# Score products of full array height: the keys' lo parts stacked twice, and smaller raw weight and temporary buffers

## The chip, the cores and the metric

The kernel runs on one core of a Trainium2 chip. The metric is the device time of one execution in microseconds (us), median of several runs. Engine names are those of the profile: PE (TensorE, its weight loads shown apart as PEld), DVE (VectorE), ACT (ScalarE), POOL (GpSimd) and SP (SyncE, which here only issues DMAs).

## The reference: what is computed

A two-layer backbone over 512 latent tokens and 256 context tokens of 1024 features. Each layer is a half SwiGLU step, an attention mixer with 16 heads of 64 features, and a second half SwiGLU step. Mixer 0 is a neighbourhood attention, mixer 1 a windowed attention with 4 key heads; both also look at all context keys. Everything is float32.

```python
def ffn_sublayer(h, shift, scale, gate, w_in, w_out, g, b):
    y = swiglu(modulate(h, shift, scale), w_in, w_out)
    return layer_norm(ALPHA * h + FFN_RES * gate * y, g, b)
...
        s_win = jnp.einsum('bcqhd,bicjhd->bhcqij', q_r, k_r).astype(jnp.float32) + bias
        s_ctx = jnp.einsum('bcqhd,bkhd->bhcqk', q_r, kc).astype(jnp.float32)
        p = jax.nn.softmax(jnp.concatenate([s_win, s_ctx], axis=-1), axis=-1).astype(v.dtype)
```

## The kernel before

Features lie on the 128 partitions, tokens along the free axis. To keep float32 accuracy with the fast float32r matmul, every large operand x is split in two float32r parts, hi (x rounded) and lo (x minus hi), and a product is a sum of three: hi·hi, hi·lo, lo·hi (`mm3`, lines 115 to 117).

**Weights** come as units of 1 MB (`wunit`). A unit arrives in two halves of 128x1024 in raw tiles `wr` (tag "wr", two of them); from each half two quarters of 128x512 are made: ACT copies the hi part `wh` (line 100), POOL subtracts to get the lo part `wl` (line 101). There are nine `wh` and nine `wl` tiles. All loads stand in one queue, SP's, in program order, and a load waits there until its buffer is free.

**A head has 64 features**, half of the array's 128 rows. The queries of a head are stacked to full height by `stack_q`: hi above lo for the even head of a pair, lo above hi for the odd one. `stack_k` makes, for each head, a tile `nk` (in mixer 1 `wk`) with the hi part of the keys in both halves, and one tile `nkl` (`wkl`) for both heads with their lo parts, each in its own half. A score product is then two matmuls (`scores`, lines 526 and 527; in mixer 1's window 816 and 817): the full-height one, (q_hi + q_lo)·k_hi, and one of half height, 64 rows, q_hi·k_lo:

```python
nc.tensor.matmul(ps, q[:, qc], k[:, kc], start=True, stop=False)
nc.tensor.matmul(ps, q[own, qc], kl[own, kc], start=False, stop=True)
```

Here `own` is the half in which the head's hi part lies. Of such pairs mixer 0 has 160 (`lat`, 128, and `cself`, 32) and mixer 1 has 128, all with 128 query columns as weights and 256 moving key columns, but for 32 of mixer 1 that have 384.

**After the scores** of a head, DVE takes the row minimum (the scores are negated), ACT the exponential, POOL scales (line 565), PE transposes (line 549), ACT or DVE copies out of PSUM, and PE multiplies with the values (line 558). Score banks have the PSUM tag "s", two of them.

**Buffers in SBUF.** Stacked queries and keys, pieces of modulation weights (`wt`, read by DVE's products on line 173) and some temporaries share the tag "slab" with 10 tiles; a quad of mixer 0's heads takes 2 x 5 of them. Temporaries have the tags "t2" (7 tiles) and "ln" (3). In `layer_norm` the squares of the centred tiles go to "ln" tiles, and POOL and DVE add them; the last outputs `ot` use "ln" for feature tiles 0 to 2 and "t2" for the others.

**Order.** The program is written once; a list scheduler with its own model of the engines then orders the instructions on each engine's queue. Each engine runs its queue in order. `bias_tables` puts 8 DMAs `xd` and 16 DMAs `yd` of 252 KB into SP's queue in the second chunk of the first SwiGLU step.

Of the kernel before, what the change touches and what calls it, by code (L numbers as in the profile page):

```python
# [8 lines left out]
F32 = mybir.dt.float32  # L9
# [9 lines left out]
P = 128  # L19
D = 1024  # L20
DT = D // P
NL = 512
# [8 lines left out]
NH = 16  # L31
RW = 63
# [3 lines left out]
def hybrid_kernel(ctx: ExitStack, tc: tile.TileContext, h0, cc, crow, wmod, wmodt, bmod, lnp, wst,  # L36
# [46 lines left out]
    wpos, loaded = [0], [None]  # L83

    def wunit(slabs=False, again=None):
        i = wpos[0] if again is None else again
        if again is None:
            wpos[0] += 1
        hs, ls = [], []
        for s in range(2):  # L90
            raw = wp.tile([P, 1024], F32, tag="wr", name=f"wr{i}_{s}" + ("" if again is None else "b"), bufs=2)
            loaded[0] = nc.sync.dma_start(raw[:], wst[i, :, s * 1024:(s + 1) * 1024])
            for q in range(2):
                nm = f"{i}_{2 * s + q}" + ("" if again is None else "b")
                if slabs:
                    hi, lo = [sp.tile([P, 512], F32R, tag="slab", name=f"w{x}{nm}", bufs=10) for x in "hl"]
                else:
                    hi, lo = [wp.tile([P, 512], F32R, tag=f"w{x}", name=f"w{x}{nm}", bufs=9) for x in "hl"]
                src = raw[:, q * 512:(q + 1) * 512]
                nc.scalar.copy(hi[:], src)  # L100
                nc.gpsimd.tensor_tensor(out=lo[:], in0=src, in1=hi[:].bitcast(F32), op=ALU.subtract)  # L101
                hs.append(hi)
                ls.append(lo)
# [21 lines left out]
    def gemv(layer, ch, pieces, tag):  # L125
        """silu(c) @ w_mod + b_mod for 512 columns (chunk ch of the host's layout), both streams, features on partitions."""
        nm = f"{layer}_{ch}"
        ps = bank(tag, f"gm{nm}")
        kt = 0
        for t in pieces:  # L130
            for j in range(t.shape[1]):
                q = kt % 4
                nc.tensor.matmul(ps[32 * q:32 * q + 32, :], c_sb[:, kt, :], t[:, j, :], start=kt < 4, stop=kt >= 4,
                                 tile_position=(0, 32 * q))
                kt += 1
        ev = t2(f"gev{nm}")
        nc.scalar.copy(ev[:], ps[:])
        pt = bank(tag, f"gt{nm}")
        for j in range(4):
            nc.tensor.matmul(pt[:, 2 * j:2 * j + 2], ev[:, j * P:(j + 1) * P], sel[:], start=True, stop=True)  # L140
        for a in range(2):
            t = ch * 2 + 8 * a if ch < 4 else ch * 4 + 2 * a
            nc.vector.tensor_tensor(out=mod[layer][:, t:t + 2, :], in0=pt[:, 4 * a:4 * a + 4].rearrange("p (t s) -> p t s", s=2),
                                    in1=bmod_sb[:, layer, t:t + 2, None].broadcast_to([P, 2, 2]), op=ALU.add)

    def gemv_bg(layer, ch):
        pieces = []
        for q in range(8):
            t = sp.tile([P, 1, 512], F32, tag="slab", name=f"wm{layer}_{ch}_{q}", bufs=10)
# [6 lines left out]
    def gemv_dve(layer, t0, t1):  # L156
        """the same for feature tiles t0:t1 as rows of products that VectorE sums, in steps that tick() issues"""
        cb = []

        def start():  # L160
            for i in range(4):
                t = sp.tile([P, 512], F32, tag="slab", name=f"cb{layer}_{t0}_{i}", bufs=10)
# [4 lines left out]
        def products(acc, t, half):  # L167
            w = sp.tile([P, 512], F32, tag="slab", name=f"wt{layer}_{t}_{half}", bufs=10)
# [34 lines left out]
    def derive(layer, ln, mlayer, m, q=None):  # L203
        """Scales and biases of the modulated LN output: u = zn*sc + bi, alpha*h = zn*ag + ab."""
# [25 lines left out]
    def rows(t):  # L230
        """512 grid tokens in column-major order, seen in row-major order"""
        return t.rearrange("p (c r) -> p r c", r=8)

    def rowm(t):
        """512 grid tokens in row-major order, as rows and columns"""
        return t.rearrange("p (r c) -> p r c", c=64)

    def mod_out(nm, d, c0, c1, st, prm, rm=False, dd=None):
        """zn (in z) -> u hi/lo (row-major if rm) and alpha*h (in z)"""
# [11 lines left out]
        else:  # L251
            uf = sp.tile([P, 512], F32, tag="slab", name=f"uf{nm}_{d}", bufs=10)
# [10 lines left out]
    def keep(d, c0, c1, prm, rm=False):  # L263
        """z = alpha*h; with rm in row-major order from then on, in the room of the tile before"""
# [12 lines left out]
    def behind(x, y):  # L277
        """issue x after y if they run on the same engine"""
# [7 lines left out]
    def rstd(nm, ve, n):  # L286
        """1/sqrt(ve) by Newton's iteration from a guess on the bits"""
# [14 lines left out]
    def total(nm, n, src, split):  # L302
        """sum of the eight tiles that src(d) gives: the first on Pool, the others on DVE"""
# [16 lines left out]
    def spread(nm, y, n, tag):  # L320
        """[P, n] tile pr with pr[:, j*128 + t] = y[t, j]"""
# [5 lines left out]
    def layer_norm_pe(nm, c0, c1, tags):  # L327
        """layer_norm with TensorE's sums, for when it has nothing else to do"""
# [24 lines left out]
    def layer_norm(nm, c0, c1, tag):  # L353
        """z -> z - mean in place for columns c0:c1; returns a function that multiplies tile d by rstd."""
# [35 lines left out]
    def flush():  # L390
        """the deferred alpha*h"""
# [8 lines left out]
    def ffn(nm, groups, gt, mid, post, units=(), opened={}, head=None, apart=None):  # L400
        """z += gt * swiglu(u); mid() runs first, post(gi) after a group is complete. The first products may be there."""
# [85 lines left out]
    def wo_pairs(nm, w, os, groups, gt, tags, base=0):  # L487
        """z += gt * (o of two pairs of heads, in tiles that begin with column base) @ w_o rows"""
# [16 lines left out]
    def slab(nm):  # L505
        return sp.tile([P, NT], F32R, tag="slab", name=nm, bufs=10)
# [3 lines left out]
    def stack_q(q0, q1, c0, c1, src, scale):  # L510
        """two heads' scaled queries: [hi; lo] for head 0, [lo; hi] for head 1"""
# [5 lines left out]
    def stack_k(k0, k1, kl, c0, c1, src):  # L517
        """two heads' keys: [hi; hi] each, and the lo parts of both"""
        for k, own, other in ((k0, LOW, HIGH), (k1, HIGH, LOW)):
            nc.scalar.copy(k[own, c0:c1], src[own, :])  # L520
# [3 lines left out]
    def scores(h, ps, q, k, kl, qc, kc):  # L524
        own = (LOW, HIGH)[h]
        nc.tensor.matmul(ps, q[:, qc], k[:, kc], start=True, stop=False)
        nc.tensor.matmul(ps, q[own, qc], kl[own, kc], start=False, stop=True)

    def v_tiles(nm, w, js=range(NT // P), tags=("mm",)):
        """value tiles [128 tokens, 256]"""  # L530
# [13 lines left out]
    def transpose(nm, p, order, tags):  # L544
        """tile p = the transposes of its 128-column pieces, in that order"""
# [8 lines left out]
    def pv_mm(po, terms):  # L554
        """po[64h:64h+64] = sum of v^T p^T over key tiles, the two heads side by side; terms[i][h] = (v, p^T)"""
# [32 lines left out]
    def na_mixer(gt, ctx_ln, post):  # L588
        def proj(qd):
            i0 = wpos[0]  # L590
            ws = [None, None]
            qk = [[slab(f"n{x}{qd}_{pr}") for x in ("q0", "q1", "k0", "k1", "kl")] for pr in range(2)]

            def half(pr, c0, c1, again=None):
# [9 lines left out]
                stack_k(*sl[2:5], c0, c1, ps)  # L604
# [26 lines left out]
        def lat(qd, pr, st, oh, ol, cbs=range(4)):  # L631
# [15 lines left out]
            for cb in cbs:  # L647
                pts = []
                qc = slice(cb * P, (cb + 1) * P)
                for h in range(2):  # L650
                    nm = f"{qd}_{pr}_{cb}_{h}"
                    ps = bank("s", f"s{nm}")
                    scores(h, ps[:, 256:512], sl[h], sl[2 + h], sl[4], qc, slice(NL, NT))
                    scores(h, ps[:, 0:256], sl[h], sl[2 + h], sl[4], qc, slice(KS[cb], KS[cb] + 256))
# [17 lines left out]
        def cself(qd, pr, st, oh, ol):  # L672
# [3 lines left out]
            for h in range(2):  # L676
                nm = f"{qd}_{pr}_c_{h}"
                ps = bank("s", f"s{nm}")
                for b in range(2):
                    scores(h, ps[:, b * 256:(b + 1) * 256], sl[h], sl[2 + h], sl[4], slice(NL + b * P, NL + (b + 1) * P),  # L680
# [64 lines left out]
    def wa_mixer(gt, ctx_ln, post):  # L745
# [9 lines left out]
        def rope(nm, ps, scale):  # L755
            """rotary of scale * ps, as a float32 tile"""
# [14 lines left out]
        ks = [[slab(f"wk{x}_{i}") for x in ("0", "1", "l")] for i in range(2)]  # L771
# [23 lines left out]
        def attn(s, q, oh, ol, bs=range(4)):  # L795
# [8 lines left out]
            for b in bs:  # L804
# [8 lines left out]
                for h in range(2):  # L813
                    own = (LOW, HIGH)[h]
                    pb = bank("s", f"sw{nm}_{h}")
                    nc.tensor.matmul(pb[:, 0:nw], q[h][:, qc], k[h][:, k0:k1], start=True, stop=False)
                    nc.tensor.matmul(pb[:, 0:nw], q[h][own, qc], k[2][own, k0:k1], start=False, stop=False)
# [5 lines left out]
                    scores(h, pb2, q[h], k[h], k[2], qc, slice(NL, NT))  # L823
# [73 lines left out]
    def open_av():  # L897
        """banks for the products of chunk 0 that start before all of u is there: [half][group] = (a, v)"""
# [89 lines left out]
def _tokens(a):  # L988
    """(tokens, 1024) -> (128, 8, tokens): features on partitions"""
# [3 lines left out]
def _k_unit(w):  # L993
    """(1024, 256) -> (128, 8*256)"""
# [3 lines left out]
def _r_unit(w):  # L998
    """(256, 1024) -> (128, 4 column quarters, 2 row tiles, 256)"""
# [110 lines left out]
```

## Time and profile before

| what | value |
|---|---|
| median of 3 runs | 2991.55 us (2989.05 to 2994.65) |
| profiled execution: span from first to last instruction | 2994.0 us; no other time of it is listed |
| busy share: PE, PEld, DVE, ACT, POOL | 97%, 84%, 62%, 34%, 42% |
| mean granted TensorE clock | 0.980 |
| first SwiGLU step with the start | 0 to about 620 us |
| mixer 0 | about 620 to 1080 us |
| SwiGLU, SwiGLU | about 1080 to 2230 us |
| mixer 1 | about 2230 to 2567 us |
| last SwiGLU step | about 2567 to 2994 us |

In the timeline a row has the start in us, the duration in us, the engine, the line, the operation, what it writes and reads, and its shape (rows*columns of the array, then partitions x elements of the operand that streams). A duration of a matmul includes its way through the array, so matmuls overlap in the record; what one costs in a full stream is the distance from its start to the start of the next.

### The profile page before, as it was taken

The numbers are of one execution on the slowest core, as the hardware profiler recorded it, in microseconds if no ns is written. First come the engines' busy times: TensorE is split into PE (matmuls) and PEld (weight loads), VectorE is DVE, ScalarE is ACT, GpSimd is POOL, SyncE is SP. The second block draws the span as 40 slices with busy tenths as digits, with TensorE's granted clock in tenths as the row PEclk, the third lists the DMA queues.
The fourth block names the chain that finished last, engine by engine and source line by source line (L and its number), as shares of the span: only waits on it lengthen the run. The fifth ranks groups of instructions, "written<-read, shape, count | busy, mean of one in ns | idle before, by whom it ended". The sixth has DMA issues, their size and how long they took to land. (4 is left out here: it accounts for less than half of the span.)

```text
span 2994.0 us, 48485 instructions
## 1 busy us (share of the span) xinstructions
PE 2900.1 (97%) x18106; PEld 2502.0 (84%) x18106; DVE 1843.8 (62%) x5023; ACT 1009.5 (34%) x2082; POOL 1248.1 (42%) x1102
## 2 busy tenths in 40 slices
PE   8899999999999979999999999999999999899998
PEld 5788888887887869888888888888887677799997
DVE  3498983475444585777775767776267566733335
ACT  4122222364343453121213522222245444533333
POOL 4233333573333454232335633332466343644453
PEclk9999999999999989999999999999998899899998
DMA  7545442221111222343332323332231000233332
GB/s 287 155 137 152 134 131 70 86 96 50 54 54 46 80 74 67 109 124 107 126 106 90 107 89 120 113 120 74 82 97 57 29 29 29 64 92 93 99 106 85
DMA packets 114860, 285.98 MB, mean 96 GB/s; under 512 B 20288, under 2 KB 32704, under 8 KB 113600
## 3 DMA queue, kind: packets, MB, share of 16 engines
q1 hardware_dynamic: 114336, 282.74, 30.1%
q8 instruction: 142, 2.33, 0.3%
q14 instruction: 94, 0.77, 0.1%
q10 hardware_dynamic: 288, 0.14, 0.0%
HBM read 280.74 MB, written 6.48 MB: 96 GB/s over the span
## 5 line engine op out<-in xcount | busy, mean ns | idle before, releaser
L101 POOL TENSOR_TENSOR wl<-wr,wh 128x512 fp32r<-128x512 f32 x632 | 836.4, 1339 | 1245.8 <-ACT wh L100 967.7
L100 ACT CAST wh<-wr 128x512 fp32r<-128x512 f32 x632 | 383.0, 620 | 694.9 <-DMA wr<-in_wst_dram 307.9
L173 DVE CUSTOM_DVE_ANT_0 jk<-wt,cb 128x256 f32<-128x256 f32 x960 | 507.0, 567 | 0.0
L396 DVE SCALAR_TENSOR_TENSOR z<-pd1a,gt,z 128x512 f32<-128x512 f32 (+1 forms) x168 | 103.2, 619 | 83.7 <-PE pd1a L117 83.4
L396 DVE SCALAR_TENSOR_TENSOR z<-pd0a,gt,z 128x512 f32<-128x512 f32 (+1 forms) x168 | 102.9, 619 | 83.6 <-PE pd0a L117 83.0
L396 DVE SCALAR_TENSOR_TENSOR z<-pd0b,gt,z 128x256 f32<-128x256 f32 (+1 forms) x176 | 104.7, 600 | 66.4 <-PE pd0b L117 64.9
L115 PE MATMUL pa0a<-uh,wh 128*128 128x512 f32 (+1 forms) x328 | 113.3, 345 | 11.7 <-ACT wh L100 8.2
L115 PE MATMUL pd0a<-gh0a,wh 128*128 128x512 f32 (+1 forms) x336 | 114.6, 344 | 2.5 <-DVE z L396 2.5
L116 PE MATMUL pd0b<-gl0b,wh 128*128 128x256 f32 (+1 forms) x352 | 116.7, 332 | 0.0
L115 PE MATMUL pd0b<-gh0b,wh 128*128 128x256 f32 (+1 forms) x352 | 116.6, 334 | 0.0
L117 PE MATMUL pd0b<-gh0b,wl 128*128 128x256 f32 (+1 forms) x352 | 116.4, 332 | 0.0
L115 PE MATMUL pa1a<-uh,wh 128*128 128x512 f32 (+1 forms) x336 | 114.5, 341 | 1.3 <-DVE uh L260 1.2
L116 PE MATMUL pv1a<-ul,wh 128*128 128x512 f32 (+1 forms) x336 | 114.3, 340 | 0.0
L115 PE MATMUL pv1a<-uh,wh 128*128 128x512 f32 (+1 forms) x336 | 114.3, 340 | 0.0
L116 PE MATMUL pd0a<-gl0a,wh 128*128 128x512 f32 (+1 forms) x336 | 114.3, 340 | 0.0
L116 PE MATMUL pd1a<-gl1a,wh 128*128 128x512 f32 (+1 forms) x336 | 114.2, 340 | 0.0
L117 PE MATMUL pd0a<-gh0a,wl 128*128 128x512 f32 (+1 forms) x336 | 114.2, 340 | 0.0
L116 PE MATMUL pa1a<-ul,wh 128*128 128x512 f32 (+1 forms) x336 | 114.2, 340 | 0.0
L117 PE MATMUL pa1a<-uh,wl 128*128 128x512 f32 (+1 forms) x336 | 114.1, 340 | 0.0
L117 PE MATMUL pd1a<-gh1a,wl 128*128 128x512 f32 (+1 forms) x336 | 114.0, 340 | 0.0
L117 PE MATMUL pv1a<-uh,wl 128*128 128x512 f32 (+1 forms) x336 | 114.0, 339 | 0.0
L115 PE MATMUL pd1a<-gh1a,wh 128*128 128x512 f32 (+1 forms) x336 | 113.6, 342 | 0.0
(880 smaller groups left out, 9246.3 us busy)
## 6 DMA issues: line engine op xcount, KB each, us to landing
wr<-in_wst_dram SPq DMA_DIRECT2D x316, 512.0 KB
wt<-in_wmodt_dram SPq DMA_DIRECT2D x240, 256.0 KB
wr_0b<-in_wst_dram SPq DMA_DIRECT2D x19, 512.0 KB
wr_1b<-in_wst_dram SPq DMA_DIRECT2D x19, 512.0 KB
wm<-in_wmod_dram SPq DMA_DIRECT2D x8, 1024.0 KB
nb<-yd SPq DMA_DIRECT2D x60, 128.0 KB
wm<-in_wmod_dram SPq DMA_DIRECT2D x16, 256.0 KB
yd<-xd SPq DMA_DIRECT2D x16, 252.0 KB
```

The lines of the kernel that those rows point to most:

```text
L100: nc.scalar.copy(hi[:], src)
L101: nc.gpsimd.tensor_tensor(out=lo[:], in0=src, in1=hi[:].bitcast(F32), op=ALU.subtract)
L115: nc.tensor.matmul(ps, a[0], b[0], start=first, stop=False)
L116: nc.tensor.matmul(ps, a[0], b[1], start=False, stop=False)
L117: nc.tensor.matmul(ps, a[1], b[0], start=False, stop=last)
L173: x = nc.vector.tensor_tensor_reduce(out=junk[:, 0:256], in0=w[:, q * 256:q * 256 + 256], in1=cb[2 * st + half][:, q * 256:q * 256 + 256], ...
L396: last[0] = nc.vector.scalar_tensor_tensor(out=zt(d, c0, c1), in0=pd, scalar=gt[:, d, st:st + 1], in1=zt(d, c0, c1), op0=ALU.mult, op1=ALU ...
```

## The change

It does five things.

1. `stack_k` makes a lo tile for each head (`nl`, in mixer 1 `wkl0`, `wkl1`), and a new ACT copy puts the lo part into the other half as well, so that the lo keys stand there twice. The second matmul of a score product takes all 128 rows: (q_hi + q_lo)·k_lo. The product lo·lo, left out before, is thereby added.
2. A quad of mixer 0 takes 2 x 6 slabs and mixer 1's keys 2 x 4; the tag "slab" has 12 tiles (`SLABS`).
3. A weight unit arrives in four quarters of 128x512, each in a raw tile of its own, three raw tiles in all: 3 x 512 elements a partition instead of 2 x 1024.
4. "t2" has 6 tiles and "ln" has 2.
5. Comments are gone, so some line numbers move: the load of `wr` from 92 to 94, the split from 100 and 101 to 99 and 100, the three products of `mm3` from 115, 116, 117 to 114, 115, 116; the score products stay on 526 and 527.

```diff
-        return tp.tile([P, 512], F32, tag=tag, name=nm, bufs={"t2": 7, "ln": 3, "sl": 2}[tag])
+        return tp.tile([P, 512], F32, tag=tag, name=nm, bufs={"t2": 6, "ln": 2, "sl": 2}[tag])
...
-        for s in range(2):
-            raw = wp.tile([P, 1024], F32, tag="wr", name=f"wr{i}_{s}" + ("" if again is None else "b"), bufs=2)
-            loaded[0] = nc.sync.dma_start(raw[:], wst[i, :, s * 1024:(s + 1) * 1024])
-            for q in range(2):
+        for q in range(4):
+            nm = f"{i}_{q}" + ("" if again is None else "b")
+            raw = wp.tile([P, 512], F32, tag="wr", name=f"wr{nm}", bufs=3)
+            loaded[0] = nc.sync.dma_start(raw[:], wst[i, :, q * 512:(q + 1) * 512])
...
-    def stack_k(k0, k1, kl, c0, c1, src):
-        for k, own, other in ((k0, LOW, HIGH), (k1, HIGH, LOW)):
+    def stack_k(k0, k1, kl0, kl1, c0, c1, src):
+        for k, kl, own, other in ((k0, kl0, LOW, HIGH), (k1, kl1, HIGH, LOW)):
             nc.scalar.copy(k[own, c0:c1], src[own, :])
             nc.scalar.copy(k[other, c0:c1], src[own, :])
             nc.vector.tensor_tensor(out=kl[own, c0:c1], in0=src[own, :], in1=k[own, c0:c1].bitcast(F32), op=ALU.subtract)
+            nc.scalar.copy(kl[other, c0:c1], kl[own, c0:c1].bitcast(F32))
...
-        nc.tensor.matmul(ps, q[own, qc], kl[own, kc], start=False, stop=True)
+        nc.tensor.matmul(ps, q[:, qc], kl[:, kc], start=False, stop=True)
...
-                    nc.tensor.matmul(pb[:, 0:nw], q[h][own, qc], k[2][own, k0:k1], start=False, stop=False)
+                    nc.tensor.matmul(pb[:, 0:nw], q[h][:, qc], k[2 + h][:, k0:k1], start=False, stop=False)
```

The scheduler's order on PE and DVE stays nearly what it was; three places show what moves.

On PE, a stretch of mixer 0 in which the score products of the second pair of heads stand between query products `pq` of the next quad's projection (numbers at a name's end tell buffers apart). Before:

```order
L115 MATMUL pq_0_0_8608<-uh_106,wh_3_8604 128x512
L526 MATMUL s_1_0_0_8337<-nk_1_7448,nq_1_7446 128x256
L527 MATMUL s_1_0_0_8337<-nkl_1_7450,nq_1_7446 128x256
L526 MATMUL s_1_0_0_8337<-nk_1_7448,nq_1_7446 128x256
L527 MATMUL s_1_0_0_8337<-nkl_1_7450,nq_1_7446 128x256
L116 MATMUL pq_0_0_8608<-ul_114,wh_3_8604 128x512
L117 MATMUL pq_0_0_8608<-uh_106,wl_3_8605 128x512
```

Now (`nl` is the new lo tile of one head):

```order
L115 MATMUL pk_0_0_8843<-ul_108,wh_0_8792 128x512
L526 MATMUL s_1_0_0_8537<-nk_1_7623,nq_1_7621 128x256
L527 MATMUL s_1_0_0_8537<-nl_1_7625,nq_1_7621 128x256
L526 MATMUL s_1_0_0_8537<-nk_1_7623,nq_1_7621 128x256
L527 MATMUL s_1_0_0_8537<-nl_1_7625,nq_1_7621 128x256
L116 MATMUL pk_0_0_8843<-uh_100,wl_0_8793 128x512
```

The four score products stand together between projection products of the next quad as before, a few rows further on (among its key products `pk`), in the same number; only the lo operand is another.

On ACT, the first call of `stack_k` (`pk` is the PSUM bank with the keys, `wh` are weight quarters, `sql` squares of the layer norm). Before:

```order
L520 CAST nk_0_6296<-pk_0_0_6471 64x512
L521 CAST nk_0_6296<-pk_0_0_6471 64x512
L362 ACTIVATE sql_1_1_6320<-z_92 128x256
L362 ACTIVATE sql_1_2_6324<-z_93 128x256
L362 ACTIVATE aql_1_1_6316<-z_94 128x256
L362 ACTIVATE sql_1_4_6330<-z_95 128x256
L100 CAST wh_2b<-wr_1b 128x512
L362 ACTIVATE sql_1_5_6334<-z_96 128x256
L520 CAST nk_0_6297<-pk_0_0_6471 64x512
L521 CAST nk_0_6297<-pk_0_0_6471 64x512
```

Now:

```order
L519 CAST nk_0_6440<-pk_0_0_6621 64x512
L520 CAST nk_0_6440<-pk_0_0_6621 64x512
L99 CAST wh_2b<-wr_2b 128x512
L361 ACTIVATE sql_1_5_6480<-z_96 128x256
L361 ACTIVATE sql_1_6_6484<-z_97 128x256
L99 CAST wh_3b<-wr_3b 128x512
L522 CAST nl_0_6442<-nl_0_6442 64x512
L519 CAST nk_0_6441<-pk_0_0_6621 64x512
L520 CAST nk_0_6441<-pk_0_0_6621 64x512
```

The new copy (line 522, `nl` from `nl`) stands between the two hi copies of the first head and those of the second, with four other instructions in between, behind a subtraction of DVE that it needs.

On SP, the place where the bias tables are fetched (`wr` are raw weight pieces, `wt` modulation weights for DVE). Before:

```order
L92 DMA wr_0_844<-in_wst_dram 128x1024
L92 DMA wr_1_854<-in_wst_dram 128x1024
L582 DMA xd<-in_rpbp_dram 16x63x8 x8
L169 DMA wt_27_0_1237<-in_wmodt_dram 128x512
L169 DMA wt_27_1_1255<-in_wmodt_dram 128x512
L92 DMA wr_0_1431<-in_wst_dram 128x1024
L584 DMA yd<-xd 128x1x504 x16
L169 DMA wt_28_0_1277<-in_wmodt_dram 128x512
L92 DMA wr_1_1441<-in_wst_dram 128x1024
L92 DMA wr_0_1451<-in_wst_dram 128x1024
```

Now:

```order
L94 DMA wr_0_864<-in_wst_dram 128x512
L94 DMA wr_1_870<-in_wst_dram 128x512
L94 DMA wr_2_876<-in_wst_dram 128x512
L94 DMA wr_3_882<-in_wst_dram 128x512
L582 DMA xd<-in_rpbp_dram 16x63x8 x8
L168 DMA wt_28_0_1301<-in_wmodt_dram 128x512
L168 DMA wt_28_1_1327<-in_wmodt_dram 128x512
L168 DMA wt_29_0_1349<-in_wmodt_dram 128x512
L584 DMA yd<-xd 128x1x504 x16
L94 DMA wr_0_1455<-in_wst_dram 128x512
L94 DMA wr_1_1461<-in_wst_dram 128x512
L94 DMA wr_2_1467<-in_wst_dram 128x512
```

Before, the first half of the seventh weight unit (the second `wr_0`) stood ahead of the 16 DMAs `yd`; now all four quarters of that unit stand behind them, and three `wt` loads instead of two ahead.

More of the change, by code (lines that the diff above doesn't have):

```diff
@@ L31 @@
 NH = 16
+SLABS = 12
 RW = 63
@@ L89, in wunit @@
         hs, ls = [], []
-        for s in range(2):
-            raw = wp.tile([P, 1024], F32, tag="wr", name=f"wr{i}_{s}" + ("" if again is None else "b"), bufs=2)
-            loaded[0] = nc.sync.dma_start(raw[:], wst[i, :, s * 1024:(s + 1) * 1024])
-            for q in range(2):
[L94 to L103, printed above, removed]
+        for q in range(4):
+            nm = f"{i}_{q}" + ("" if again is None else "b")
+            raw = wp.tile([P, 512], F32, tag="wr", name=f"wr{nm}", bufs=3)
+            loaded[0] = nc.sync.dma_start(raw[:], wst[i, :, q * 512:(q + 1) * 512])
+            if slabs:
+                hi, lo = [sp.tile([P, 512], F32R, tag="slab", name=f"w{x}{nm}", bufs=SLABS) for x in "hl"]
+            else:
+                hi, lo = [wp.tile([P, 512], F32R, tag=f"w{x}", name=f"w{x}{nm}", bufs=9) for x in "hl"]
+            nc.scalar.copy(hi[:], raw[:])
+            nc.gpsimd.tensor_tensor(out=lo[:], in0=raw[:], in1=hi[:].bitcast(F32), op=ALU.subtract)
+            hs.append(hi)
+            ls.append(lo)
         return hs, ls
@@ L148, in gemv_bg @@
         for q in range(8):
-            t = sp.tile([P, 1, 512], F32, tag="slab", name=f"wm{layer}_{ch}_{q}", bufs=10)
+            t = sp.tile([P, 1, 512], F32, tag="slab", name=f"wm{layer}_{ch}_{q}", bufs=SLABS)
             nc.sync.dma_start(t[:], wmod[ch, q // 4, :, q % 4:q % 4 + 1, :])
@@ L161, in start @@
             for i in range(4):
-                t = sp.tile([P, 512], F32, tag="slab", name=f"cb{layer}_{t0}_{i}", bufs=10)
+                t = sp.tile([P, 512], F32, tag="slab", name=f"cb{layer}_{t0}_{i}", bufs=SLABS)
                 nc.sync.dma_start(t[:], crow[i // 2, i % 2:i % 2 + 1, :].broadcast_to([P, 512]))
@@ L167, in products @@
         def products(acc, t, half):
-            w = sp.tile([P, 512], F32, tag="slab", name=f"wt{layer}_{t}_{half}", bufs=10)
+            w = sp.tile([P, 512], F32, tag="slab", name=f"wt{layer}_{t}_{half}", bufs=SLABS)
             nc.sync.dma_start(w[:], wmodt[layer, t, half])
@@ L251, in mod_out @@
         else:
-            uf = sp.tile([P, 512], F32, tag="slab", name=f"uf{nm}_{d}", bufs=10)
+            uf = sp.tile([P, 512], F32, tag="slab", name=f"uf{nm}_{d}", bufs=SLABS)
         uo, uv, lo, zv = uh[d][:, c0:c1], uf[:, :n], ul[d][:, c0:c1], zs
@@ L505, in slab @@
     def slab(nm):
-        return sp.tile([P, NT], F32R, tag="slab", name=nm, bufs=10)
+        return sp.tile([P, NT], F32R, tag="slab", name=nm, bufs=SLABS)
     LOW, HIGH = slice(0, 64), slice(64, 128)
@@ L591, in proj @@
             ws = [None, None]
-            qk = [[slab(f"n{x}{qd}_{pr}") for x in ("q0", "q1", "k0", "k1", "kl")] for pr in range(2)]
+            qk = [[slab(f"n{x}{qd}_{pr}") for x in ("q0", "q1", "k0", "k1", "l0", "l1")] for pr in range(2)]
             def half(pr, c0, c1, again=None):
@@ L603, in half @@
                 mmk(ps, ws[pr], P, c0, c1)
-                stack_k(*sl[2:5], c0, c1, ps)
+                stack_k(*sl[2:6], c0, c1, ps)
             if qd == 0:
@@ L770, in wa_mixer @@
         w = wunit()
-        ks = [[slab(f"wk{x}_{i}") for x in ("0", "1", "l")] for i in range(2)]
+        ks = [[slab(f"wk{x}_{i}") for x in ("0", "1", "l0", "l1")] for i in range(2)]
         for i in range(2):
@@ L822, in attn @@
                     pb2 = bank("c", f"sc{nm}_{h}")[:, 0:NC] if split else pb[:, nw:nw + NC]
-                    scores(h, pb2, q[h], k[h], k[2], qc, slice(NL, NT))
+                    scores(pb2, q[h], k[h], k[2 + h], qc, slice(NL, NT))
                     if split:
```

10 lines of the change are left out of this document (4 added, 6 removed).

## The prediction

> **What bounds the kernel now.** I read the page's first part, then the busy time by stretch (660 to 1080 us is mixer 0, 2285 to 2565 mixer 1, from 2560 the last SwiGLU), then the waits. In the stretches the columns are length, then busy us of PE, PEld, DVE, ACT and POOL, then the granted clock, the DMA share and GB/s.
>
> ```profile
> PE 2900.1 (97%) x18106; PEld 2502.0 (84%) x18106; DVE 1843.8 (62%) x5023; ACT 1009.5 (34%) x2082; POOL 1248.1 (42%) x1102
> 660.00:1080.00 420.00, 417.63 (x2746) 334.13 (x2746) 216.62 (x586) 176.78 (x415) 166.36 (x180) 1.00 0.20 60
> 2285.00:2565.00 280.00, 275.97 (x1689) 198.56 (x1688) 166.12 (x417) 134.55 (x377) 116.55 (x145) 0.93 0.11 35
> 2560.00:2994.00 434.00, 407.22 (x3323) 401.83 (x3319) 191.10 (x428) 153.52 (x307) 214.69 (x179) 0.96 0.30 93
> ```
>
> PE sets the pace: in the two mixers it is idle for 2.4 us of 420 and 4.0 of 280, while no other engine is busy above 60%. So what shortens PE's stream there shortens the kernel, until another engine's chain takes over. But a busy PE need not stream at full rate. The timeline tells, by the distance from start to start: first full-height products of 256 columns in the first SwiGLU, then mixer 0's score products.
>
> ```profile
> 563.11 0.28 PE L116 MATMUL pa0a<-ul,wh 128*128 128x256 f32 x1
> 563.23 0.28 PE L117 MATMUL pa0a<-uh,wl 128*128 128x256 f32 x1
> 563.35 0.28 PE L115 MATMUL pa0a<-uh,wh 128*128 128x256 f32 x1
> ...
> 810.38 0.39 PE L115 MATMUL pq<-uh,wh 128*128 128x512 f32 x1
> 810.61 0.28 PE L526 MATMUL s<-nk,nq 128*128 128x256 f32 x1
> 810.82 0.38 PE L527 MATMUL s<-nkl,nq 64*128 64x256 f32 x1
> 811.13 0.38 PE L526 MATMUL s<-nk,nq 128*128 128x256 f32 x1
> 811.44 0.38 PE L527 MATMUL s<-nkl,nq 64*128 64x256 f32 x1
> 811.75 0.50 PE L116 MATMUL pq<-ul,wh 128*128 128x512 f32 x1
> 812.09 0.40 PE L117 MATMUL pq<-uh,wl 128*128 128x512 f32 x1
> ```
>
> Full-height products of 256 columns follow each other at 0.12 us, and 512 columns take 0.23 (810.38 to 810.61). As soon as a half-height product (64*128) is a neighbour, each takes 0.21 to 0.31, and the first 512-column product behind them 0.34. Nothing releases PE there: it waits for no other engine. The weight loads say why:
>
> ```profile
> 563.11 0.19 PEld L117 LDWEIGHTS pa0a<-uh,wl 128*128 128x128 f32 x1
> ...
> 810.82 0.18 PEld L527 LDWEIGHTS s<-nkl,nq 64*128 64x128 f32 x1 [0.24 <-issue]
> 811.13 0.19 PEld L526 LDWEIGHTS s<-nk,nq 128*128 128x128 f32 x1
> ```
>
> The load for the product of 563.23 ran from 563.11, during the product before. At 810.82 and 811.13 the load starts only with its own product's record, behind the product before it, so 0.18 us of load lie bare at each change of height.
>
> **The score products: the gain.** The change makes every product full height and removes these changes of height. How many pairs there are:
>
> ```profile
> L527 PE MATMUL s<-nkl,nq x128: 377/381/384, 663.2 to 1062.1; 64*128 64x256 f32 x128
> L527 PE MATMUL s_c<-nkl,nq x32: 377/381/382, 695.9 to 1029.4; 64*128 64x256 f32 x32
> L527 PE MATMUL sw<-wkl,wq x32: 379/380/580, 2298.7 to 2550.5; 64*128 64x256 f32 x32
> L527 PE MATMUL sc<-wkl,wq x32: 277/381/579, 2298.9 to 2541.8; 64*128 64x256 f32 x32
> L817 PE MATMUL sw<-wkl,wq x64: 379/435/686, 2288.9 to 2549.9; 64*128 64x256 f32 x32, 64*128 64x384 f32 x32
> ...
> 2343.02 0.44 PE L816 MATMUL sw<-wk,wq 128*128 128x384 f32 x1
> 2343.39 0.44 PE L817 MATMUL sw<-wkl,wq 64*128 64x384 f32 x1
> 2343.76 0.23 PE L819 MATMUL sw<-mkb,idb 128*128 128x128 bf16 x1
> ```
>
> From 810.61 to 812.09 two pairs and the product behind them took 1.48 us. At the full-height rates this is 4 x 0.12 + 0.23 = 0.71. Saved: 0.77, or 0.385 a pair. Mixer 0 has 128 + 32 = 160 pairs: 61.6 us. Mixer 1 has 32 + 32 + 32 = 96 pairs of 256: 37.0. Its 32 pairs of 384 take 0.74 now (2343.02 to 2343.76); midway between 0.12 and 0.23 a full-height 384 is 0.175, so a pair is 0.35 and saves 0.39: 12.5. Sum: 111 us, 61.6 and 49.5. Mixer 1 ran at a mean clock of 0.93, so its part could be up to 49.5/0.93 = 53: upper end 115.
>
> The Trainium skill, "TensorE: Matmul & The Clock Gate", Part 3 (what overlaps and what doesn't), would deny this: a weight load overlaps a running matmul only if it goes to other row groups, so full-height neighbours should leave their loads bare as well. By that rule a full-height pair would cost about what a mixed one does, and the sum would be near nothing. The rows at 563 us, all rows of the array in both neighbours, disagree.
>
> **What of the gain is lost to other chains.** A head's way from scores over DVE, ACT and POOL back to PE does not get shorter. The waits (total us, times, longest) show who is late:
>
> ```profile
> DVE m L657 <- PE s L527: 41.8, 43, 3.5
> DVE m L829 <- PE sw L527: 24.9, 26, 3.3
> ```
>
> In mixer 0, DVE stood waiting for the scores in 43 of 64 blocks, so PE is the late one; and projections fill PE between. There I take a loss of 4 us (0 to 12). In mixer 1 it waited in 26 of 64 only; DVE has 166 us of work in 280, and would be at 166/230 of the shorter stretch. I take a third of 49.5, 16 us, from between nothing and all of it. Late next are there DVE's reductions and the copies of the transposes. Loss 20 (0 to 60).
>
> **The new copies.** `stack_k` is called 16 times in mixer 0 and 4 times in mixer 1, two copies each:
>
> ```profile
> L520 ACT CAST nk<-pk x32: 352/474/583, 632.6 to 985.7; 64x512 fp32r<-64x512 f32 x16, 64x256 fp32r<-64x256 f32 x16
> L520 ACT CAST wk<-snk x4: 616/618/621, 2267.0 to 2276.0; 64x512 fp32r<-64x512 f32 x4
> ```
>
> 32 x 0.47 + 8 x 0.62 at most = 20 us of ACT, spread over stretches in which ACT is busy 177 of 420 us: hidden. What shows is the longer way to the first scores: DVE's subtraction, then one more copy, 0.6 us, at the starts of the four quads and of mixer 1. 5 x 0.6 = 3 us (0 to 12, if it showed at all 20 calls). ACT stands in order behind that copy, and so do the weight copies `wh`; they have the lead of nine tiles.
>
> **The raw tiles.** The place is the bias tables, in the timeline:
>
> ```profile
> 114.51 15.95 SPq L584 DMA_DIRECT2D yd<-xd  x16
> ...
> 132.59 1.68 SPq L92 DMA_DIRECT2D wr<-in_wst_dram  x2
> ...
> 134.76 0.40 PE L117 MATMUL pd0a<-gh0a,wl 128*128 128x512 f32 x1
> 143.34 0.79 PE L115 MATMUL pa0a<-uh,wh 128*128 128x512 f32 x1 [8.18 <-ACT wh L100]
> ```
>
> Now PE waits 8.2 us for the half unit issued behind the tables. In the new order the whole unit stands behind them. PE's order makes up for part: three more tiles of down products stand ahead of the unit's first product; but the 13 products of 512 columns that used the unit's first half before the wait now stand behind it. 13 x 0.23 = 3 us lost, if the loads land when they did (0 to 8, the wait once more). Elsewhere smaller loads are neutral in the sum; the rival below prices them. SP has 354 more issues, all in the shade of PE.
>
> **The smaller "t2", "ln" and larger "slab" tags.** With two "ln" tiles the fourth square of a layer norm must wait for POOL's first addition. The nearest row is POOL's 128x512 tensor-tensor operation at 1.34 us; PE waited for a norm's result seven times:
>
> ```profile
> L101 POOL TENSOR_TENSOR wl<-wr,wh 128x512 fp32r<-128x512 f32 x632 | 836.4, 1339 | 1245.8 <-ACT wh L100 967.7
> PE prl L324 <- DVE yl L294: 19.5, 7, 6.2
> ```
>
> 7 x 1.34 = 9 at most, nothing if the additions are ahead; I take 2, since centring on DVE goes on meanwhile. At the very end the third output tile must wait for the first one's DMA:
>
> ```profile
> 2987.13 0.60 ACT L961 ACTIVATE ot<-zspare,lnp_sb 128x256 f32<-128x256 f32 x1 [6.13 <-DVE zspare L348]
> 2987.75 3.75 SPq L962 DMA_DIRECT2D out_dram<-ot  x8
> 2987.81 1.84 ACT L961 ACTIVATE ot<-z,lnp_sb 128x256 f32<-128x256 f32 x3
> ```
>
> The last issue ends at 2991.5 and the span at 2994.0, so a landing takes up to 2.5 us; the first one's at 2990.2 lets ACT's other three tiles (1.84 us) end at 2992.1 instead of 2989.65: 2 us (0 to 3). More slabs let modulation weights come earlier; DVE, which reads them, is off PE's path: nothing, and the same if they came late.
>
> **Sum.** -111 + 20 + 3 + 3 + 2 + 2 = -81 on the profiled execution's 2994.0 us (its span; no further time of it is shown), which stands 2.45 us above the median of 2991.55. So 2991.55 - 81 = 2910.5.
>
> **Rivals.** (A) Full height does not make the products cheaper: what costs is something else in scores, such as a new pair of operands each time. Then only the costs without the 20 stay, 10 us: 3001; with a saving of 0.04 a pair (load 0.18 and stream 0.11 bare, 0.58 against 0.62) it is 2990. For it speaks that no full-height score product has a full-height neighbour among the scores; against it the 0.12 at 563 us, where operands change as often. Chance 0.04. The Trainium skill, "TensorE: Matmul & The Clock Gate", section "Why this matters for your kernels", points the way of A: a single matmul with few rows takes as long as one with all 128. The trace agrees for one record, 0.38 us each, and not for the distance to the next.
>
> (B) Mixer 1, and part of mixer 0, is bound by the softmax chain as soon as PE is faster. For it: DVE waits for scores in fewer than half of mixer 1's blocks. Against it: DVE is busy 59% there. Nothing from mixer 1 and 12 lost in mixer 0: -61.6 + 12 + 10 = -40, 2952. Chance 0.05.
>
> (C) Slower: three raw tiles of a quarter starve the weight stream in the last SwiGLU. Its 11 chunks of 3 units, 3 repeated and 2 repeated units are 38 units or 152 quarters in 407 us of PE, 2.7 us each. A raw tile is taken for issue to landing, plus 0.62 (ACT's split, a copy like those above) and 1.34 (POOL's). Three tiles keep pace up to 8.1 us, a landing of 6.1; the outputs above landed within 2.5. From 9.7 us, 3.23 a quarter, 152 x 0.53 = 81 us eat the gain. At 11 us a cycle it is 152 x 0.97 = 147 lost: 3058. Against it: PE is idle for 27 us only in that stretch, with two raw tiles of a half unit, and nine split tiles of each kind are a reserve. Chance 0.04.
>
> The forecast, a gain of 50 to 115, has 0.87. For the range: all of 115 and no costs is 2876; nothing from mixer 1 but a whole mixer 0, -61.6 + 10, is 2940. 2876 to 2940 leaves out A, B and C, 0.13. Faster by over 0.2% (6 us, about what runs of this kernel that differ by 0.2% around their median can tell from no change): 0.92, forecast and B; within: 0.02; slower: 0.06, C and half of A.
>
> **What would show it.** In the profile after, score products of line 526 and 527 start 0.12 us apart and their loads start one product ahead; mixer 0 ends about 58 us earlier in its own length, mixer 1 about 30 to 35 shorter; PE there waits at transposes for POOL, at line 558 for copies, some 20 us more; PE's wait near 130 to 145 us grows by a few us. The prediction is wrong if the distance stays near 0.3, if mixer 1 keeps its length with PE idle, or if PE waits for `wh` or `wl` in SwiGLU stretches.

## The result, and the profile after

The changed kernel takes 2929.59 us (median of 4 runs, 2926.03 to 2932.93) against 2992.99 for the kernel before on the same chip (4 runs, 2989.05 to 2994.65): a ratio of 0.9785, 95% interval 0.9771 to 0.9799, 2.15% faster (the two medians alone differ by 63.4 us). The prediction was 2910.5, range 2876 to 2940. The profiled execution has a span of 2924.2 us, 69.7 less than before; a run's time is 1.8 us above its span.

The timeline of PE and of its weight loads in mixer 0, after, at four score products of one block (start, duration, engine, line, operation):

```profile
812.17 0.28 PE L116 MATMUL pq<-uh,wl 128*128 128x256 f32 x1
812.29 0.28 PE L526 MATMUL s<-nk,nq 128*128 128x256 f32 x1
812.41 0.28 PE L527 MATMUL s<-nl,nq 128*128 128x256 f32 x1
812.53 0.27 PE L526 MATMUL s<-nk,nq 128*128 128x256 f32 x1
812.64 0.28 PE L527 MATMUL s<-nl,nq 128*128 128x256 f32 x1
812.76 0.60 PE L549 MATMUL tp<-idn,p 128*128 128x128 f32 x4
...
812.29 0.19 PEld L527 LDWEIGHTS s<-nl,nq 128*128 128x128 f32 x1
812.41 0.19 PEld L526 LDWEIGHTS s<-nk,nq 128*128 128x128 f32 x1
```

Score products now follow each other at 0.12 us, and the load for the product of 812.41 starts at 812.29, with the product before it. That is the step on which the prediction stood. The rule of the Trainium skill that it was weighed against ("TensorE: Matmul & The Clock Gate", Part 3) is not borne out: both neighbours use all rows of the array, and their loads overlap.

The busy time by stretch: length, busy us of PE, PEld, DVE, ACT, POOL, granted clock, DMA share, GB/s. First mixer 0 (first score to last product with values) and mixer 1 of before, then the same two after.

```profile
661.70:1073.22 411.52, 410.39 (x2691) 327.51 (x2691) 210.81 (x570) 172.36 (x403) 162.57 (x176) 1.00 0.20 61
2288.60:2563.10 274.50, 271.24 (x1661) 194.91 (x1661) 161.39 (x407) 130.65 (x368) 112.95 (x142) 0.93 0.11 35
```
```profile
669.23:1032.26 363.03, 355.28 (x2694) 310.45 (x2694) 209.18 (x571) 184.93 (x431) 162.63 (x176) 1.00 0.25 71
2253.73:2491.86 238.13, 227.46 (x1660) 179.59 (x1661) 163.25 (x410) 134.13 (x376) 114.66 (x144) 0.99 0.14 41
```

Mixer 0 is 48.5 us shorter and mixer 1 36.4: 84.9 us, 15 more than the span lost. In mixer 1 the granted clock moved too, from 0.93 to 0.99, so not all of its 36.4 need be height. The rest was given back elsewhere. The first score of mixer 0 starts at 669.23, no longer at 661.70: 7.5 us later. Between the two mixers (1073.22 to 2288.60 before, 1032.26 to 2253.73 after) 6.1 us more pass, and behind mixer 1 another 1.5. The longest single wait in it is the one at the bias tables, 8.18 us before and 10.94 in the timeline after:

```profile
118.22 15.27 SPq L584 DMA_DIRECT2D yd<-xd  x16
134.27 3.03 SPq L94 DMA_DIRECT2D wr<-in_wst_dram  x3
...
145.12 0.79 PE L114 MATMUL pa0a<-uh,wh 128*128 128x512 f32 x1 [10.94 <-ACT wh L99]
```

So two questions: is it the height that gives the 85 us, and what costs the 15?

### The profile page after: what moved, and what is told of

It is laid out like the page before. It is cut to its first block, busy times and chain, and to the rows that moved or that the text cites. A ratio compares the mean times of both kernels' runs of the same rounds, so it can differ in the third digit from the quotient of the medians.

```text
span 2924.2 us, 49325 instructions
## 1 busy us (share of the span) xinstructions
PE 2802.8 (96%) x18106; PEld 2470.4 (84%) x18106; DVE 1842.5 (63%) x5023; ACT 1033.0 (35%) x2122; POOL 1247.8 (43%) x1102
## 5 line engine op out<-in xcount | busy, mean ns | idle before, releaser
L99 ACT CAST wh<-wr 128x512 fp32r<-128x512 f32 x632 | 388.9, 620 | 738.4 <-DMA wr<-in_wst_dram 324.4
L172 DVE CUSTOM_DVE_ANT_0 jk<-wt,cb 128x256 f32<-128x256 f32 x960 | 489.3, 544 | 0.0
```

Of the source, the lines that this page charges most:

```text
L99: nc.scalar.copy(hi[:], raw[:])
L172: x = nc.vector.tensor_tensor_reduce(out=junk[:, 0:256], in0=w[:, q * 256:q * 256 + 256], in1=cb[2 * st + half][:, q * 256:q * 256 + 256], ...
```

## Experiments

Ratios are to the kernel before on the same chip, with 95% intervals. 1% is 30 us.

**Height alone.** The changed kernel with the second product at 64 rows again (the line in `scores`; the one in mixer 1's window is changed in the same way):

```diff
...
-        nc.tensor.matmul(ps, q[:, qc], kl[:, kc], start=False, stop=True)
+        nc.tensor.matmul(ps, q[own, qc], kl[own, kc], start=False, stop=True)
```

> The changed kernel with its second score product at half height again (64 rows, lo times lo left out as in the kernel before); the new lo tiles, their mirror copies, 12 slabs, the three quarter raw tiles and the smaller temporary tags all stay. Theory (the array height is what changed the time): score products go back to 0.2 to 0.31 us apart with bare weight loads, and what the change costs elsewhere (7.5 us up to the first score of mixer 0, about 5 in the SwiGLU stretches between the mixers, both from the traces of before and after) stays: 3000 to 3008 us, some 0.3 to 0.5% over before. Rival (the time came from the other parts, such as more slabs or smaller loads that reach PE earlier): it stays near 2930.

3016.92 us, ratio 1.0076 (1.0057 to 1.0094). Height is what makes the kernel faster: 0.9785/1.0076 = 0.9711, or 87 us, with some 7 of uncertainty. The rest of the change costs 0.76%, 23 us (17 to 28), more than the 7.5 + 5 that the two traces had suggested. Its stretches, mixer 0 and mixer 1:

```profile
669.52:1084.20 414.68, 411.84 (x2694) 328.11 (x2694) 213.20 (x571) 186.09 (x431) 162.29 (x176) 1.00 0.21 62
2305.59:2578.05 272.46, 266.55 (x1660) 190.79 (x1661) 164.91 (x410) 134.85 (x376) 114.79 (x144) 0.97 0.12 36
```

From here to the changed kernel PE's busy time falls by 56.6 us in mixer 0 and 39.1 in mixer 1, and its idle time grows from 2.8 to 7.8 and from 5.9 to 10.7. In length 51.7 and 34.3 are left, 86.0 together.

**Is it the change of height, or the half-height product itself?** The kernel before, the products of a mixer 0 block regrouped: two of full height, then two of half height (the same for `cself`, not shown):

```diff
-                    scores(h, ps[:, 256:512], sl[h], sl[2 + h], sl[4], qc, slice(NL, NT))
-                    scores(h, ps[:, 0:256], sl[h], sl[2 + h], sl[4], qc, slice(KS[cb], KS[cb] + 256))
+                    scores2(h, ps, sl[h], sl[2 + h], sl[4], (qc, qc), (slice(KS[cb], KS[cb] + 256), slice(NL, NT)))
...
+    def scores2(h, ps, q, k, kl, qcs, kcs):
+        own = (LOW, HIGH)[h]
+        for i in range(2):
+            nc.tensor.matmul(ps[:, i * 256:(i + 1) * 256], q[:, qcs[i]], k[:, kcs[i]], start=i == 0, stop=False)
+        for i in range(2):
+            nc.tensor.matmul(ps[:, i * 256:(i + 1) * 256], q[own, qcs[i]], kl[own, kcs[i]], start=False, stop=i == 1)
```

> The kernel before with mixer 0's four score products of a block in another order: two of full height, then two of half height, so that a block has two changes of height where it had four (the scheduler keeps most of these groups). Nothing else is changed. Theory (a change of height costs 0.19 us, the bare weight load, whichever way it goes): 80 blocks x 2 changes x 0.19 = 31 us less in mixer 0, 25 to 31 with the groups that the scheduler splits: about 2964. Half-height neighbours would then start 0.12 apart. Variant (only full-height neighbours hide the load, two half-height ones on the same rows do not): half of it, 15 us, about 2978. Rival (a product of half height costs 0.3 us itself, or a new pair of operands does): no gain, 2991 to 2995.

2967.83 us, ratio 0.9906 (0.9891 to 0.9921): 28 us faster with the same 160 half-height products, the size that the price of 0.19 for a change of height gave. The distances from each score product of mixer 0 to the next start on PE, without idle time, add up to 66.8 us in this trace and to 95.0 in that of before: the 28 us lie there. The kernel's timeline (532 full, 534 half height, `x2` two products in a row):

```profile
800.40 0.39 PE L532 MATMUL s<-nk,nq 128*128 128x256 f32 x2
800.73 0.50 PE L534 MATMUL s<-nkl,nq 64*128 64x256 f32 x2
801.16 0.51 PE L116 MATMUL pq<-ul,wh 128*128 128x512 f32 x1
...
800.73 0.29 PEld L534 LDWEIGHTS s<-nkl,nq 64*128 64x128 f32 x2
```

The four take 801.16 - 800.40 = 0.76 us where they took 1.14 before (810.61 to 811.75 in the prediction's rows). The expectation's picture is wrong inside, though: two half-height neighbours are not 0.12 apart but 0.22 (median of 72 such pairs in this trace), while a change costs 0.21 behind two products of one height and 0.31 where heights alternate. So a half-height product costs something by itself, and a change of height in every product was the dearest order; that the sum came out inside the theory's 25 to 31 is in part luck. The Trainium skill, "TensorEngine Tiling (Array Packing)", section Key Properties, says that a change of tiling mode drains the TensorE. The trace agrees that such a change costs, 0.21 to 0.31 us against 0.12, but it has 0.22 between two half-height neighbours as well, where no mode changes. The Trainium skill gives no price there.

**Where the 23 us come from.** The kernel before with only the smaller buffers, then with parts of them: three quarter raw tiles alone, `ln` 2 alone, `t2` 6 alone, and all of them with 12 slabs.

```diff
-        ... bufs={"t2": 7, "ln": 3, "sl": 2}[tag])
+        ... bufs={"t2": 6, "ln": 2, "sl": 2}[tag])
...
-            raw = wp.tile([P, 1024], F32, tag="wr", ..., bufs=2)
+            raw = wp.tile([P, 512], F32, tag="wr", ..., bufs=3)
```

> The kernel before with the smaller buffers alone: three quarter raw tiles in the place of two half tiles, six t2 and two ln tiles; ten slabs, one shared lo tile and half-height products as before. The prediction's terms: raw tiles 3, layer norms 2, tail 2: 7 us slower, about 3000. By the traces of before and after: 5 us up to the end of the first SwiGLU and 4 to 5 us in the SwiGLU stretches between the mixers, nothing at the tail: 9 to 10 us, about 3003. Rival (these microseconds come from the new copies and the order that follows them): less than 3 us, 2992 to 2996.

> The kernel before with the three quarter raw tiles alone (t2 7, ln 3, ten slabs, half-height products as before). It splits the 1.06% that the smaller buffers together cost. Theory (the raw tiles cost what the start shows, 2.9 us more at the bias tables and some us up to the first pd0a_r, and the rest comes from the temporary tags, whose layer norms, stacked queries and first scores PE waits for): 4 to 8 us over before, 1.0013 to 1.0027. Rival (the quarter loads themselves are the slower part, everywhere a unit is loaded): 20 us or more, over 1.007.

> The kernel before with all smaller buffers and with twelve slabs in the place of ten, but no lo tiles of their own and no mirror copies: between the run with the smaller buffers (1.0106) and the run with the changed kernel at half height (1.0076). Theory (two more slabs, taken from no head, let stacked tiles and modulation weights come earlier, and they give back at least what lies between those two): 1.004 to 1.0076, and the mirror copies then cost the rest up to 1.0076. Rival (slabs are worth nothing, as the prediction had it, and the order alone differs): 1.0095 to 1.012.

> The kernel before with two ln tiles in the place of three, nothing else changed. The raw tiles alone took 0.35%, all smaller buffers 1.06%, so the two temporary tags take some 0.7%, 21 us. ln holds the squares of the layer norms, the modulated inputs of feature tiles 0 to 2 and the scratch output of DVE's modulation products. Theory (ln is the short one: DVE reaches the stacked tiles at the start of mixer 0 later, 6 us there, and the norms do): 10 to 18 us over before, 1.0033 to 1.006. Rival (the prediction's term for it, 2 us, is right and t2 takes the rest): under 1.0015.

> The kernel before with six t2 tiles in the place of seven, nothing else changed. t2 holds mixer 0's and mixer 1's exponentials, and gate and norm temporaries. Theory (one tile fewer holds up ACT's exponential, and with it the score banks, in the mixers, where the run with all smaller buffers is 6.7 us longer than the one with the raw tiles alone): 5 to 10 us over before, 1.0017 to 1.0033. Rival (t2 has tiles to spare, ln takes all of the 0.7%): under 1.001.

| kernel before with | median us | ratio | 95% interval |
|---|---|---|---|
| all smaller buffers | 3029.02 | 1.0106 | 1.0089 to 1.0124 |
| quarter raw tiles alone | 3004.81 | 1.0035 | 1.0023 to 1.0047 |
| `ln` 2 alone | 2999.76 | 1.0023 | 1.0012 to 1.0033 |
| `t2` 6 alone | 2997.22 | 1.0015 | 1.0006 to 1.0024 |
| all smaller buffers, 12 slabs | 3027.06 | 1.0102 | 1.0085 to 1.0119 |

All three buffers cost something. Raw tiles take 10 us, slightly over the theory's 4 to 8 and half of what the rival said; `ln` 7, below the theory's range and above the rival's bound; `t2` 4.5, just below its range. Alone they add to 0.73%, together they take 1.06%: 0.33% more, with an uncertainty of some 0.26. In the run at half height, which has all three too, the whole rest takes 0.76%, no more than the sum, so that they make each other worse is not shown. Two more slabs are worth nothing that these runs can tell from noise, as the prediction had it. The run with lo tiles and mirror copies on top (1.0076) is not slower than the one without (1.0102): at half height the copies show no cost. It is 0.26% faster, at the edge of the intervals. In the traces a good part lies in mixer 0: with all smaller buffers it takes 421.2 us, 10.2 of them at half the granted clock, and at half height 414.7 with none at half clock (411.5 before). Why it is so stays open.

A small part of the cost shows in the waits of PE in mixer 0's run-up (total us, times, longest), before in 602 to 662 us and then with all smaller buffers in 606 to 672:

```profile
PE prl L324 <- DVE yl L294: 1.6, 1, 1.6
...
PE vn L115 <- DVE nkl L522: 0.7, 1, 0.7
```
```profile
PE prl L322 <- DVE yl L292: 2.4, 1, 2.4
PE vn L113 <- DVE nq L512: 1.9, 2, 1.5
PE vn L113 <- DVE nkl L520: 1.9, 1, 1.9
PE pq L113 <- DVE uh L258: 1.3, 1, 1.3
```

DVE is late there with the norm, the modulated input `uh` and the stacked tiles. With `ln` 2 alone the waits for `nq` (1.6 us) and `uh` (1.3) are there, with the raw tiles alone the one for `nq` (2.2), and with `t2` 6 alone the run-up waits as before; the run-up is 4 us of the 26 by which the profiled execution with all smaller buffers is longer. Where the two tags cost the rest is not shown: in these traces mixer 1 alone spends between 20 and 44 us at half clock, and that hides differences of this size. In the code `ln` also holds the first three modulated inputs of the first step and the scratch output of DVE's modulation products, and `t2` holds the exponentials `p` and `pw` of both mixers. The prediction had looked at the norms' squares and the last outputs only.

**The copies on POOL.**

```diff
-            nc.scalar.copy(kl[other, c0:c1], kl[own, c0:c1].bitcast(F32))
+        for kl, own, other in ((kl0, LOW, HIGH), (kl1, HIGH, LOW)):
+            nc.gpsimd.tensor_copy(kl[other, c0:c1], kl[own, c0:c1].bitcast(F32))
```

> The changed kernel with the mirror copies of the lo keys on POOL, issued at the end of stack_k, in the place of ACT. Theory (ACT, which waits in order for DVE's subtraction before it can copy, holds the PSUM bank of the keys and the copies queued behind it: 2.3 us at the start of mixer 0 and some of the 7.7 us that PE stands idle in mixer 0 after): 2 to 6 us faster than the changed kernel, 2924 to 2928. Rival (POOL's copy is slower than ACT's, near its 1.34 us for 128x512 against 0.6, and lies on the way to the first scores of each quad): 0.7 x 5 = 3 to 4 us slower, 2933.

2921.16 us, ratio 0.9753 (0.9740 to 0.9767), 0.32% better than the changed kernel's 0.9785. That is some 10 us with an uncertainty of 6, at or above the theory's 2 to 6; the place isn't the theory's. Up to mixer 0's first score its span is 2.3 us shorter, but 2.1 of that lie before the last product of the first SwiGLU; mixer 0 gains 0.8, mixer 1 3.2. So that ACT's queue was the reason is not shown. The rival's price was wrong: the copy takes as long on either engine, 0.50 us on POOL and 0.51 on ACT (medians over the two sizes; this kernel, then the changed one):

```profile
L523 POOL CAST nl<-nl x32: 392/502/690, 640.9 to 953.3; 64x512 fp32r<-64x512 f32 x16, 64x256 fp32r<-64x256 f32 x16
```
```profile
L522 ACT CAST nl<-nl x32: 392/512/623, 642.7 to 953.9; 64x512 fp32r<-64x512 f32 x16, 64x256 fp32r<-64x256 f32 x16
```

**The wait at the bias tables.** The DMAs `yd` written two at a time, in chunks 2 to 9 of the first SwiGLU:

```diff
+            if mid is not None and ci in range(2, 10):
+                bias_heads(2 * (ci - 2))
...
-        for h in range(NH):
+    def bias_heads(h0):
+        for h in (h0, h0 + 1):
```

> The changed kernel with the 16 DMAs yd of the bias tables issued two at a time in chunks 2 to 9 of the first SwiGLU step, not all in chunk 2. Theory (the 10.9 us that PE waits for wh near 145 us stand behind the burst of these DMAs in SP's queue; two at a time hide under a chunk of 51 us): 8 to 11 us faster than the changed kernel, and the half clock of 10 us behind that wait goes too, up to 5 more: 2914 to 2922, ratio 0.974 to 0.976. Rival (the wait is split over eight chunks and stays in sum): 2927 to 2931, ratio 0.9775 to 0.979.

2917.49 us, ratio 0.9743 (0.9727 to 0.9758): 0.42% better than the changed kernel, the size that the theory gave. What ran is not what the theory had in mind, though. SP's queue, in time:

```profile
116.95 1.33 SPq L94 DMA_DIRECT2D wr<-in_wst_dram  x3
118.38 3.69 SPq L588 DMA_DIRECT2D yd<-xd  x5
123.31 0.34 SPq L94 DMA_DIRECT2D wr<-in_wst_dram  x1
123.70 6.80 SPq L588 DMA_DIRECT2D yd<-xd  x7
130.60 0.55 SPq L94 DMA_DIRECT2D wr<-in_wst_dram  x1
131.85 0.65 SPq L588 DMA_DIRECT2D yd<-xd  x1
...
137.28 2.01 SPq L588 DMA_DIRECT2D yd<-xd  x2
```

The scheduler drew all 16 together again: they stand between 118 and 140 us, in less than the 51 us of one chunk and not over eight. But three loads of `wr` stand ahead of them now and single ones between, where the changed kernel has all 16 in a row. So it is the weight loads' place in the queue that was tried; two at a time under a chunk was not. PE's waits between 72 and 600 us, in the changed kernel and then with this edit:

```profile
PE pa0a L114 <- ACT wh L99: 10.9, 1, 10.9
PE pd0a L114 <- DVE z L395: 2.6, 5, 0.6
```
```profile
PE pd0a L114 <- DVE z L395: 4.4, 9, 1.2
PE prl L323 <- DVE yl L293: 2.4, 1, 2.4
```

The wait for weights is gone, nothing of its size took its place, and the first `pd0a_r` product at the end of this stretch starts 11.2 us earlier. With the wait went the half clock behind it: 10.2 us from 139.4 in the changed kernel, none between 72 and 596 us here. Of the 11.2 us, 9.7 are left at the end of the span.

**Both.** 

> The changed kernel with both: mirror copies on POOL and the DMAs yd two at a time. If the two gains lie at different places, they add: 8 us from the one and 8 to 16 from the other, 2906 to 2914, ratio 0.970 to 0.9725. If one takes the place of the other, or POOL's wl copies come late behind the mirror copies: 2918 to 2922, ratio 0.974 to 0.9755.

2913.41 us, ratio 0.9727 (0.9713 to 0.9740). This is the fastest version here, 0.58% better than the changed kernel. Over the spread DMAs alone it gains 0.16% with an uncertainty of 0.2, so the two gains don't clearly add.

**Two raw tiles.** On top of both, `wr` with two quarter tiles, and the space given to `ln` 3 or to `t2` 7.

> The changed kernel with the mirror copies on POOL and the DMAs yd two at a time, and with a third ln tile, paid for by two quarter raw tiles in the place of three. If ln is short and two raw tiles keep pace (a landing of 2.5 us plus 0.6 and 1.3 is 4.4 us a tile, so two tiles feed a quarter every 2.2 us against the 2.7 that PE needs): 8 to 15 us faster than with both changes alone, 2898 to 2906, ratio 0.968 to 0.970. If the raw tiles starve the weights, PE waits for wh in the SwiGLU stretches and it is slower than 2913, by up to 81 us or more.

> As the run with a third ln tile, but the space of the third raw tile goes to a seventh t2 tile. If t2 is the short tag and two raw tiles keep pace: 5 to 10 us faster than with both changes alone, 2903 to 2908, ratio 0.969 to 0.971. If two raw tiles starve the weights, both runs of this pair are slower by the same.

2944.27 us, ratio 0.9844 (0.9830 to 0.9858), and 2945.80, 0.9850 (0.9836 to 0.9864). Both are 1.2% slower than the version they start from; the pair moves together, so it is the raw tile. The last SwiGLU up to its last product, with two raw tiles and then with three, and below each, over the whole kernel, ACT's split of the weights (busy, mean ns | idle before it, and what ended most of that):

```profile
2512.86:2920.62 407.76, 391.36 (x3191) 386.26 (x3190) 173.49 (x345) 137.05 (x273) 201.27 (x164) 0.98 0.33 94
...
L99 ACT CAST wh<-wr 128x512 fp32r<-128x512 f32 x632 | 391.8, 620 | 999.1 <-DMA wr<-in_wst_dram 653.1
```
```profile
2501.54:2892.81 391.27, 385.69 (x3191) 383.43 (x3192) 165.60 (x344) 139.31 (x272) 200.21 (x164) 0.98 0.33 98
...
wr<-in_wst_dram SPq DMA_DIRECT2D x632, 256.0 KB, 3.1
...
L99 ACT CAST wh<-wr 128x512 fp32r<-128x512 f32 x632 | 388.4, 620 | 732.2 <-DMA wr<-in_wst_dram 319.1
```

That stretch grows by 16.5 us, and over the whole kernel ACT stands waiting for landings 653 us, no longer 319. In that stretch PE waits 5.6 us for `wh` and `wl`, with three tiles 0.6; its busy time grows too, by 5.7. The expectation took a landing of 2.5 us; the page with three tiles has a median of 3.1 from issue to landing. With 0.6 and 1.3 a tile is then taken for 5.0, two tiles deliver a quarter every 2.5 us against the 2.7 that PE needs, and that leaves next to nothing for a landing that is late (an estimate; how late the landings are with two tiles, the trace does not tell). This is the prediction's rival C, with its threshold one tile lower.

## Why the prediction was right

The time came out 19 us above the forecast and inside its range, through the mechanism that it named. By its own steps:

| term | predicted | measured | from |
|---|---|---|---|
| score products, mixer 0 | -61.6 | -56.6 | PE busy, half height to full |
| score products, mixer 1 | -49.5 | -39.1 | the same |
| chain loss, mixer 0 | +4 | +4.9 | PE idle 2.8 to 7.8 |
| chain loss, mixer 1 | +16 | +4.8 | PE idle 5.9 to 10.7 |
| copies, raw tiles, `ln`/`t2`, tail | +10 | +23 (17 to 28) | ratio at half height |
| sum | -81 | -63 | medians |

**Height net of the loss:** -91 predicted, -87 measured. That it came so near is in part luck, for two errors cancel in mixer 1. PE's busy time fell by 10 us less than forecast, and some 5 of the 39.1 are clock, not height (mixer 1 spent 17 us at half clock in the half-height run and 7 after; in the kernel before it was 37.5, so that of the 36.4 us by which mixer 1 is shorter than there, an estimated 15 are clock); its chain lost 11 us less than the third that was taken. The price of 0.385 a pair came from the densest place, two pairs between projection products: 0.33 a pair at the score products and 0.055 at the product behind them. Adding up in the traces the distance from each score product to the next start on PE, without idle time, gives 95.1 us in mixer 0 at half height and 44.1 after: 0.32 a pair, nearly the price. The products right behind the scores add up to 17.8 us and 12.6 after: 0.03 a pair, not 0.055. Nearly half of the runs of score products (38 of 86) are followed not by a projection but by a transpose or by an `o` product of half the array's width (128*64), where less or nothing is saved: from an `o` product to the next one of full width it is 0.20 us, before and after.

**The chain.** DVE waits for scores less often after, in mixer 0 and in mixer 1:

```profile
DVE m L657 <- PE s L527: 13.6, 17, 3.1
```
```profile
DVE m L828 <- PE sw L527: 8.9, 8, 1.6
```

17 times where it was 43, and 8 where it was 26. So the chains moved towards being the late side, as said, but PE became idle for only 9.7 us more in the two mixers, not 20. Its waits there are scattered, the longest 1.6 us; they lie near transposes and line 558, as expected, and at the score banks. Rival B needed PE idle for all that its products saved in mixer 1.

**The step that was mis-sized** is "The smaller t2, ln and larger slab tags": 2 us, from the squares of seven norms, with its upper bound at 9. Alone the two tags take 11 to 12 us, with the raw tiles on top about 21 (1.06% less 0.35%), and in the run at half height some 12 (0.76% less 0.35%). The step had followed the squares and the last outputs only; all users of a tag count. The raw tiles' 3 us, bounded at 8, were 10. At the place that was named they were sized rightly: the wait at the bias tables grew by 2.8 us, from 8.18 to 10.94. What failed is "Elsewhere smaller loads are neutral": with the raw tiles alone the stretch between the mixers is already 6.1 us longer, as much as in the changed kernel. The slabs were nothing, as said. The 2 us for the output tile at the end did not show: from the last product of the last norm to the end of the span it is 0.2 us more.

**Rivals.** A (full height makes nothing cheaper, 2990 to 3001) is refuted by the run at half height, 3017 against 2930. C did not happen with three raw tiles and did with two.

## What to carry to other kernels

Price a matmul by the distance between starts and by its neighbours: here 64 rows cost more than 128, because the weight loads around a half-height product lay bare: 0.31 us from start to start where heights alternate, 0.21 to 0.22 when grouped, 0.12 at full height. Where the operand can't be made full height, group products of one height; that took 28 us out of this kernel and needed no buffer. When a change is paid for in buffers, list every user of each tag that shrinks, and measure the shrunken buffers without the change: here the rest of the change took back 23 of the 87 us that the height gave.

## What the runs showed of the hardware

PE's granted clock can fall to a half behind waits, and a few waits can then cost more through it than by themselves. Before, behind the first blocks of mixer 1, and after, at the same place; then the kernel with all smaller buffers in mixer 0, a wait and the 10.2 us behind it:

```profile
2305.60:2339.80 34.20, 32.93 (x126) 21.56 (x126) 15.99 (x45) 15.26 (x49) 12.37 (x17) 0.50 0.10 32
2339.80:2374.00 34.20, 33.69 (x222) 24.20 (x222) 16.41 (x41) 14.43 (x38) 12.12 (x15) 1.00 0.09 28
```
```profile
2276.10:2283.00 6.90, 6.53 (x37) 5.22 (x34) 5.54 (x15) 5.01 (x18) 4.81 (x6) 0.51 0.38 107
```
```profile
704.96 0.55 PE L524 MATMUL s_c<-nk,nq 128*128 128x256 f32 x1 [1.17 <-ACT p L660]
```
```profile
705.03:715.27 10.24, 10.24 (x40) 7.22 (x41) 4.95 (x11) 6.10 (x16) 2.79 (x6) 0.50 0.00 0
```

126 products in 34.2 us at clock 0.50, 222 in the next 34.2 at 1.00; PE counted as busy in both. After, the half clock lasted 6.9 us, at half height 10.2 at that place, in the regrouped kernel mixer 1 had 44 us of it in all. Not every wait does it: one of 1.54 us at 671 us of the changed kernel left the clock at full. The Trainium skill, "TensorE: Matmul & The Clock Gate", Part 1, has the clock follow PE's recent activity, judged in windows of about 3.4 us; the stretches here agree (3.4, 6.8, 10.2 and 34.1 us). The Trainium skill has the clock fall after a whole idle window; there the trace differs: the drop at 705 us came behind 1.17 us of waiting. Why before stayed low for ten windows, while PE was busy for 96% of them, no run here shows.
